# Six raw weight buffers instead of four, and three split tiles instead of four, in a two-block transformer kernel

## The chip, the cores and the metric

One NeuronCore of a Trainium2 chip. The metric is the device time of one execution in microseconds. PE is TensorE (matrix products), DVE is VectorE, ACT is ScalarE, POOL is GpSimd, SP the engine whose queue issues the weight loads.

## What is computed

256 tokens of width 1024, all in float32, pass through two blocks. The first has two layers, each a half-weighted SwiGLU FFN (width 2816), a mixer (attention with convolution in layer 0, a gated recurrence in layer 1) and a second FFN. The second block modulates each part by a condition (shift, scale and gate), and has a mixer and a dense FFN, then a mixer and a mixture of eight experts, of which each token takes two. The parts that fill the time are all of this form:

```python
def _swiglu_2(h, w_gate, w_up, w_down):
    return (jax.nn.silu(h @ w_gate) * (h @ w_up)) @ w_down
```

## The kernel before

**Split products.** PE does not multiply float32 at full precision in one pass, so each weight is split in two: ACT copies it to the reduced format (`wh`, the high part, line 222 as called from `split`), and DVE subtracts that from the original (`wl`, the low part, line 231). The tokens are split in the same way. `mm3` (lines 327 to 336) makes three products of them: high by high (L333), low tokens by high weight (L334), high tokens by low weight (L336).

**Pieces.** Weights come in pieces of 1 MB, 128 partitions by 2048 columns. `load` (L298 to L301) takes a buffer of the pool `raw` and issues the transfer on SP's queue (L300). `split` takes one `wh` and one `wl` tile from their pools and fills them, in parts of 1024 columns in the dense stages and in one of 2048 in the MoE. A raw buffer is free when DVE has read it; a pair of split tiles is free when PE has made the last product of it. Each pool hands out its buffers in turn, so the load of a piece waits for DVE to finish the piece four before it, and the split of a piece waits for PE to finish the piece four before it. In the stages that have spare memory (`ext`), one or two named slots extend the rotation: in `f10`, `f20` and `f11` a fifth pair joins the four, and `self.turn` counts the rotation.

**Stages.** f10, mx0, f20, f11, mx1, f21 (first block), b0, d0, b1, e1 (second). In a dense stage the tokens are two tiles of 128 (tile 0 and tile 1). An FFN runs over six chunks of its width (five of 512, one of 256): up and gate products, the activation, transposes, and the down products of the chunk before. In the first chunk of an FFN and in the first block of a mixer, four pieces are held while PE works tile 0 through all of them, then transposes tile 1's norm (`split_T`, L399), then works tile 1 through the four. An output projection does the same with its four pieces, tile 0 first, whose norm for the next stage then runs on DVE, ACT and POOL while PE works tile 1.

**MoE.** Each expert has 33 pieces. Experts with up to 64 tokens work with "half" blocks: high and low parts of the tokens stand side by side, so that a 1024-by-512 product needs two matmuls per 128 rows (`prod`, L428), 8 for a piece, and `glu` adds the two halves (a copy on ACT, a matmul on PE at L437). One expert of up to 128 tokens works with full blocks, 12 matmuls for a piece. The largest has room for a full block and a half block (12 + 8 = 20 matmuls for a piece); its six chunks are called between those of the others (`big_up`, `big_down`), four or two pieces at a time, so PE passes from 20 matmuls a piece to 8 twelve times. Which expert comes is known at run time alone; the order of work is fixed.

**Order on the engines.** Each engine runs its instructions in one fixed order, which a scheduler writes from the program's order and the buffers' releases. A change of a pool's size can therefore move instructions. There is no table of numbers by hand around the pools, only a few pins.

Of the kernel before, what the change touches and what calls it, by code (L numbers as in the profile page):

```python
# [192 lines left out]
class K:  # L193
    def __init__(self, ctx, tc, A, out, dbg=None):
        self.tc, self.nc, self.A, self.out, self.dbg = tc, tc.nc, A, out, dbg or {}
        e = ctx.enter_context
        self.raw_p = e(tc.tile_pool(name="raw", bufs=4))
        self.h_p = e(tc.tile_pool(name="wh", bufs=4))
        self.l_p = e(tc.tile_pool(name="wl", bufs=4))
        self.slots = e(tc.tile_pool(name="slots", bufs=1))  # L200
        self.cst = e(tc.tile_pool(name="cst", bufs=1))
        self.sm_p = e(tc.tile_pool(name="sm", bufs=1))
        self.ps = e(tc.tile_pool(name="ps", bufs=4, space=bass.MemoryType.PSUM))
        self.dr = e(tc.tile_pool(name="dr", bufs=1, space=bass.MemoryType.DRAM))
        self.n = 0
        self.ext, self.turn, self.in_moe, self.c_row = (), 0, False, None
        self.first, self.behind = True, None
        self.setup()
# [97 lines left out]
    def split(self, raw, nk, n, pin=False):  # L306

        out = []
        if self.turn < 4:
            pair = self.h_p.tile([128, 2048], F32R, tag="wh", name="wh"), self.l_p.tile([128, 2048], F32R, tag="wl", name="wl")  # L310
        else:
            pair = [self.slot(i, [128, 2048], F32R) for i in self.ext]
        self.turn = (self.turn + 1) % (5 if len(self.ext) == 2 else 4)
        hi, lo = pair
        per = nk if self.in_moe else max(1, 1024 // n)
        for k0 in range(0, nk, per):
            m = min(per, nk - k0)
            sl = slice(k0 * n, (k0 + m) * n)
            with self.tc.issue_after(self.behind.ins) if self.behind else ExitStack():
                self.act(hi[:, sl], raw[:, sl], AF.Copy)  # L320
            self.behind = None
            ins = self.tt(lo[:, sl], raw[:, sl], hi[:, sl].bitcast(F32), OP.subtract)
            if pin:
                self.pin(ins)
            out.append([tuple(v[:, k * n:(k + 1) * n] for v in pair) for k in range(k0, k0 + m)])
        return out
# [1554 lines left out]
```

## Time and profile before

| | |
|---|---|
| time of three runs | 2278.87, 2285.14, 2280.76 us; median 2280.76 |
| the profiled execution | 2283.6 us, of which the span from first to last instruction is 2281.8 |
| granted TensorE clock, mean | 0.991 of full speed |
| PE busy | 2174.7 us (95%) |
| DVE, ACT, POOL busy | 1661.9 (73%), 1303.8 (57%), 100.3 us (4%) |
| read from memory | 569.80 MB, 250 GB/s over the span |
| weight loads in the MoE | 264 of 1024 KB, 5.8 us from issue to landing in the median |

In the rows below a line such as `ACT wh L222 <- PE acc L428: 25.3, 12, 5.3` says that ACT sat idle before writing a `wh` tile until a product of line 428 was done, for 25.3 us in all, in 12 cases, at most 5.3 us. A timeline row gives the start, the length, the engine, the line and the operation, how many such instructions were run together (x2), and in brackets the idle time before it with what ended it.

### The profile page before, as it was taken

The numbers are of one execution on the slowest core, as the hardware profiler recorded it, in microseconds if no ns is written. First come the engines' busy times: TensorE is split into PE (matmuls) and PEld (weight loads), VectorE is DVE, ScalarE is ACT, GpSimd is POOL, SyncE is SP. The second block draws the span as 40 slices with busy tenths as digits, with TensorE's granted clock in tenths as the row PEclk, the third lists the DMA queues.
The fourth block names the chain that finished last, engine by engine and source line by source line (L and its number), as shares of the span: only waits on it lengthen the run. The fifth ranks groups of instructions, "written<-read, shape, count | busy, mean of one in ns | idle before, by whom it ended". The sixth has DMA issues, their size and how long they took to land.

```text
span 2281.8 us, 28012 instructions
## 1 busy us (share of the span) xinstructions
PE 2174.7 (95%) x10654; PEld 1752.4 (77%) x10654; DVE 1661.9 (73%) x1900; ACT 1303.8 (57%) x1589; POOL 100.3 (4%) x152
## 2 busy tenths in 40 slices
PE   8999999999999999999999999988999989899997
PEld 6888878888889788877888878756787666676674
DVE  5785967657657876665745666888788788887887
ACT  5455554444437644455544474777666666767675
POOL 0001010000000100120000211000000000000000
PEclk9999999999999999999999999999999999999999
DMA  8684248758755587533655432789898888889886
GB/s 325 251 331 168 104 179 328 265 185 313 274 188 171 200 314 259 207 107 129 231 185 178 165 139 102 286 331 350 295 334 321 324 324 317 328 310 341 317 313 254
DMA packets 82253, 572.82 MB, mean 251 GB/s; under 512 B 9373, under 2 KB 9685, under 8 KB 15424
## 3 DMA queue, kind: packets, MB, share of 16 engines
q1 hardware_dynamic: 77616, 556.73, 65.9%
q0 software_dynamic: 3920, 13.12, 1.8%
q8 instruction: 86, 1.41, 0.2%
q10 hardware_dynamic: 576, 1.11, 0.1%
q14 instruction: 55, 0.45, 0.1%
HBM read 569.80 MB, written 1.12 MB: 250 GB/s over the span
## 4 chain that ended last, share of the span: by engine, by line
PE 39%; DVE 9%; ACT 6%; issue 2%; DMA 1%; POOL 1%; ACTq 0%; DVEq 0%; POOLq 0%
PE mm L428 8%; DVE wl L231 7%; ACT wh L222 5%; PE mm L333 4%; PE mm L334 4%; PE mm L336 4%; PE acc L428 3%; PE acc L334 3%; PE acc L333 3%; PE acc L336 2%; DMA raw<-in_moe 1%; PE mm L1470 1%; ACT s L222 1%; PE mm L596 1%; PE mm L1585 1%
## 5 line engine op out<-in xcount | busy, mean ns | idle before, releaser
L231 DVE TENSOR_TENSOR wl<-raw,wh 128x1024 fp32r<-128x1024 f32 (+3 forms) x658 | 1065.9, 1644 | 356.5 <-ACT wh L222 354.5
L222 ACT ACTIVATE wh<-raw 128x1024 fp32r<-128x1024 f32 (+3 forms) x658 | 897.1, 1393 | 451.5 <-PE mm L334 196.0
L333 PE MATMUL mm<-wh,s 128*128 128x512 f32 (+2 forms) x1144 | 428.5, 380 | 1.6 <-ACT s L222 1.3
L334 PE MATMUL mm<-wh,s 128*128 128x512 f32 (+2 forms) x1144 | 425.3, 376 | 1.5 <-DVE s L231 1.5
L222 ACT ACTIVATE s<-mm 128x512 fp32r<-128x512 f32 (+10 forms) x445 | 225.5, 523 | 346.3 <-PE mm L428 117.0
L336 PE MATMUL mm<-wl,s 128*128 128x512 f32 (+2 forms) x1144 | 322.2, 376 | 1.9 <-DVE wl L231 1.9
L428 PE MATMUL mm<-wl,s 128*128 128x512 f32 (+1 forms) x656 | 248.6, 386 | 32.6 <-DVE wl L231 32.2
L333 PE MATMUL acc<-wh,s 128*128 128x512 f32 x680 | 270.1, 398 | 4.7 <-DVE s L231 2.8
L334 PE MATMUL acc<-wh,s 128*128 128x512 f32 x680 | 268.4, 395 | 0.8 <-DVE s L231 0.8
L333 PEld LDWEIGHTS mm<-wh,s 128*128 128x128 f32 x1144 | 216.8, 190 | 42.4 <-ACT s L222 3.1
L334 PEld LDWEIGHTS mm<-wh,s 128*128 128x128 f32 x1144 | 217.2, 190 | 40.6 <-DVE s L231 3.8
L428 PE MATMUL mm<-wh,s 128*128 128x512 f32 (+1 forms) x656 | 244.1, 380 | 0.0
L336 PEld LDWEIGHTS mm<-wl,s 128*128 128x128 f32 x1144 | 208.1, 190 | 40.6 <-DVE wl L231 2.3
L336 PE MATMUL acc<-wl,s 128*128 128x512 f32 x680 | 213.8, 393 | 0.0
L428 PEld LDWEIGHTS mm<-wl,s 128*128 128x128 f32 x656 | 124.0, 189 | 73.4 <-DVE wl L231 51.0
L333 PEld LDWEIGHTS acc<-wh,s 128*128 128x128 f32 x680 | 128.6, 190 | 32.9 <-ACT s L222 4.2
L334 PEld LDWEIGHTS acc<-wh,s 128*128 128x128 f32 x680 | 129.2, 190 | 27.1 <-DVE s L231 1.7
L336 PEld LDWEIGHTS acc<-wl,s 128*128 128x128 f32 x680 | 128.5, 190 | 26.5
L428 PEld LDWEIGHTS mm<-wh,s 128*128 128x128 f32 x656 | 124.3, 189 | 24.2 <-issue 3.8
L428 PE MATMUL acc<-wl,s 128*128 128x512 f32 x308 | 125.4, 411 | 16.6 <-DVE wl L231 16.6
L231 DVE TENSOR_TENSOR s<-mm,s 128x512 fp32r<-128x512 f32 (+5 forms) x209 | 119.7, 597 | 25.2 <-PE mm L437 12.5
L428 PE MATMUL acc<-wh,s 128*128 128x512 f32 x308 | 125.8, 411 | 2.1 <-ACT wh L222 2.1
(313 smaller groups left out, 2128.0 us busy)
## 6 DMA issues: line engine op xcount, KB each, us to landing
raw<-in_moe SPq DMA_DIRECT2D x264, 1024.0 KB, 5.8
raw<-in_f SPq DMA_DIRECT2D x132, 1024.0 KB, 6.0
raw<-in_ada_w SPq DMA_DIRECT2D x48, 1024.0 KB, 4.9
raw<-in_dense SPq DMA_DIRECT2D x33, 1024.0 KB, 4.8
raw<-in_w_in SPq DMA_DIRECT2D x12, 1024.0 KB, 4.9
raw<-in_ow_in SPq DMA_DIRECT2D x8, 1024.0 KB, 5.0
raw<-in_w_out SPq DMA_DIRECT2D x8, 1024.0 KB, 4.8
raw<-in_ew_in SPq DMA_DIRECT2D x7, 1024.0 KB, 5.0
```

Of the source, the lines that this page charges most:

```text
L222: return self.nc.scalar.activation(out=out, in_=in_, func=func, **kw)
L231: return self.nc.vector.tensor_tensor(out=out, in0=in0, in1=in1, op=op)
L333: mm(out=out, lhsT=xs[i][0], rhs=ws[i][0], start=first and i == 0, stop=False)
L334: mm(out=out, lhsT=xs[i][1], rhs=ws[i][0], start=False, stop=False)
L336: mm(out=out, lhsT=xs[i][0], rhs=ws[i][1], start=False, stop=last and i == n - 1)
L428: self.nc.tensor.matmul(out=out, lhsT=x[0], rhs=w[j][:, c0:c0 + n], start=first and k == 0 and j == 0, stop=last and k == len(ws) - 1 and ...
L596: mm(out=out, lhsT=a, rhs=b, start=j == 0, stop=j == len(todo) - 1)
L1470: mm(out=p[:, k * w:(k + 1) * w], lhsT=h[t][:, a, kk * 128:(kk + 1) * 128], rhs=one[:, o:o + w], start=t == 0, stop=t == 1)
L1585: mm(out=p, lhsT=o[:, t * 128:(t + 1) * 128], rhs=v[:, sl], start=b == 0, stop=b == len(parts) - 1)
```

## The change

The pool `raw` has six buffers instead of four, and the pools `wh` and `wl` have three tiles instead of four. All tiles are 128 by 2048 of 4 bytes, 8 KB of each partition, so the memory is the same: 4 + 4 + 4 and 6 + 3 + 3. The rotation in `split` is shortened by one to match: a split waits for PE to finish the piece three before it (four in f10, f20 and f11, five before), a load waits for DVE to finish the piece six before it.

```diff
-        self.raw_p = e(tc.tile_pool(name="raw", bufs=4))
-        self.h_p = e(tc.tile_pool(name="wh", bufs=4))
-        self.l_p = e(tc.tile_pool(name="wl", bufs=4))
+        self.raw_p = e(tc.tile_pool(name="raw", bufs=6))
+        self.h_p = e(tc.tile_pool(name="wh", bufs=3))
+        self.l_p = e(tc.tile_pool(name="wl", bufs=3))
...
-        if self.turn < 4:
+        if self.turn < 3:
...
-        self.turn = (self.turn + 1) % (5 if len(self.ext) == 2 else 4)
+        self.turn = (self.turn + 1) % (4 if len(self.ext) == 2 else 3)
```

The scheduler writes another order with it. The first place is PE at the start of e1, where the four pieces are `wh_10959`, `wh_10965`, `wh_10971` and `wh_10977` (each with the `wl` of the next number), `mm_10982` and `mm_11007` are tile 0's sums, `mm_11077` is one of tile 1's, and `mm_11039` and `mm_11048` are the transposes of tile 1's norm. Before:

```order
L334 MATMUL mm_11007<-wh_10977,s1_205_10843 128x512
L336 MATMUL mm_11007<-wl_10978,s0_204_10842 128x512 x4
L399 MATMUL mm_11039<-ident_81,s11_206_10844 128x128 x4
L399 MATMUL mm_11048<-ident_81,s11_206_10844 128x128 x4
L1391 MATMUL mm_11058<-rtr_7051,s0_204_10842 128x16 x4
L333 MATMUL mm_11077<-wh_10959,s0_204_10842 128x512
```

With the change, PE around the same transposes:

```order
L336 MATMUL mm_11007<-wl_10972,s0_216_10842 128x512 x4
L399 MATMUL mm_11039<-ident_81,s11_218_10844 128x128 x4
L399 MATMUL mm_11048<-ident_81,s11_218_10844 128x128 x4
L1391 MATMUL mm_11058<-rtr_7051,s0_216_10842 128x16 x8
L1391 MATMUL mm_11058<-rtr_7051,s1_217_10843 128x16 x4
L333 MATMUL mm_11077<-wh_10959,s0_216_10842 128x512
```

The transposes follow the third piece now, without the fourth. Where the fourth comes in on PE, some 15 rows on:

```order
L336 MATMUL mm_11077<-wl_10960,s0_216_10842 128x512 x4
L333 MATMUL mm_11077<-wh_10965,s0_216_10842 128x512
L334 MATMUL mm_11077<-wh_10965,s1_217_10843 128x512
L333 MATMUL mm_11077<-wh_10965,s0_216_10842 128x512
L334 MATMUL mm_11077<-wh_10965,s1_217_10843 128x512
L333 MATMUL mm_11077<-wh_10965,s0_216_10842 128x512
L333 MATMUL mm_11007<-wh_10977,s0_216_10842 128x512
L334 MATMUL mm_11007<-wh_10977,s1_217_10843 128x512
```

Tile 0's products of the fourth piece (`wh_10977`) stood ahead of the transposes; they stand behind tile 1's twelve products of the first piece (`wl_10960` ends them) and five of the second. The starts of f21, b0, d0 and b1 change in the same way.

The second place is PE in the output projection of b1, ahead of e1, where the four pieces are `wh_10756`, `wh_10764`, `wh_10772` and `wh_10780`, `acc_10750` and `acc_10751` are tile 0's sums, and `acc_10752` and `acc_10753` tile 1's. Before, on PE, the end of the fourth piece for tile 0 and the beginning of tile 1:

```order
L333 MATMUL acc_10751<-wh_10780,s3_195_10448 128x512
L334 MATMUL acc_10751<-wh_10780,s10_196_10449 128x512
L336 MATMUL acc_10751<-wl_10781,s3_195_10448 128x512 x2
L333 MATMUL acc_10752<-wh_10756,s3_195_10448 128x512
L334 MATMUL acc_10752<-wh_10756,s10_196_10449 128x512
```

Tile 1 began when tile 0 had used all four. With the change, on PE, the fourth piece's beginning for tile 0:

```order
L333 MATMUL acc_10753<-wh_10764,s3_207_10448 128x512
L334 MATMUL acc_10753<-wh_10764,s10_208_10449 128x512
L333 MATMUL acc_10753<-wh_10764,s3_207_10448 128x512
L334 MATMUL acc_10753<-wh_10764,s10_208_10449 128x512
L336 MATMUL acc_10753<-wl_10765,s3_207_10448 128x512
L333 MATMUL acc_10751<-wh_10780,s3_207_10448 128x512
L334 MATMUL acc_10751<-wh_10780,s10_208_10449 128x512
L333 MATMUL acc_10751<-wh_10780,s3_207_10448 128x512
```

The fourth piece of tile 0 moved behind tile 1's work on the first piece and five products of the second. The transposes of tile 0's norm for e1 follow later (`mm_10858`, `mm_10867`). Before, on PE, near the projection's end:

```order
L333 MATMUL acc_10753<-wh_10764,s3_195_10448 128x512
L334 MATMUL acc_10753<-wh_10764,s10_196_10449 128x512
L399 MATMUL mm_10858<-ident_81,s11_206_10844 128x128 x4
L333 MATMUL acc_10753<-wh_10764,s3_195_10448 128x512
L399 MATMUL mm_10867<-ident_81,s11_206_10844 128x128 x4
L1391 MATMUL mm_10877<-rtr_7051,s0_204_10842 128x16 x4
```

One product of tile 1 stood between the two, and more behind. With the change, on PE:

```order
L333 MATMUL acc_10753<-wh_10780,s3_207_10448 128x512
L334 MATMUL acc_10753<-wh_10780,s10_208_10449 128x512
L336 MATMUL acc_10753<-wl_10781,s3_207_10448 128x512 x2
L399 MATMUL mm_10858<-ident_81,s11_218_10844 128x128 x4
L399 MATMUL mm_10867<-ident_81,s11_218_10844 128x128 x4
L1391 MATMUL mm_10877<-rtr_7051,s0_216_10842 128x16 x4
```

They stood among tile 1's products of the projection, and now stand behind its last one. The output projection of b0 changes alike. In the steady chunks of an FFN and in the half blocks of the MoE PE's order is nearly the same as before, and the weight loads stand in the same order among themselves.

## Rows read from the trace of the kernel before

**Rows 1.** busy time by stage (us from:to, its length, then by engine, clock, DMA share, GB/s)

```profile
100.00:1350.00 1250.00, 1230.93 (x6339) 1036.05 (x6337) 853.24 (x1199) 627.86 (x954) 87.79 (x125) 1.00 0.58 211
...
1490.00:2282.00 792.00, 720.03 (x3225) 535.82 (x3223) 645.44 (x448) 537.59 (x441) 0.00 (x0) 0.99 0.85 319
```

**Rows 2.** waits of ACT, 1490 to 2282 us (us in total, times, longest us)

```profile
ACT s L222 <- PE mm L428: 112.2, 62, 4.8
ACT wh L222 <- PE acc L428: 25.3, 12, 5.3
ACT wh L222 <- DMA raw<-in_moe: 22.6, 27, 2.2
```

**Rows 3.** waits of the load queue, 1490 to 2282 us

```profile
SPq L300 <- DVE wl L231: 530.8, 205, 7.6
```

**Rows 4.** waits of DVE and of PE, 1490 to 2282 us

```profile
DVE wl L231 <- ACT wh L222: 98.6, 87, 5.9
...
PE mm L428 <- DVE wl L231: 30.2, 32, 1.8
```

**Rows 5.** chain of waits, 1490 to 2282 us, by engine and line

```profile
by line: PE mm L428 20.6%; DVE wl L231 17.9%; ACT wh L222 10.4%; PE acc L428 8.1%; PE mm L333 5.3%; PE mm L336 5.1%; PE mm L334 5.1%; issue 4.5%; DMA raw<-in_moe 3.6%; PE acc L334 2.5%; PE acc L333 2.4%; PE acc L336 2.3%; PE mm L1470 2.3%; 
```

**Rows 6.** PE, timeline at five stage starts (start us, us, work, [idle before])

```profile
782.26 1.04 PE L399 MATMUL mm<-ident,s 128*128 128x128 f32 x8
...
973.43 1.23 PE L399 MATMUL mm<-ident,s 128*128 128x128 f32 x8 [1.65 <-DVE s L231]
...
1103.63 1.03 PE L399 MATMUL mm<-ident,s 128*128 128x128 f32 x8
...
1291.64 1.03 PE L399 MATMUL mm<-ident,s 128*128 128x128 f32 x8
...
1416.53 0.39 PE L333 MATMUL mm<-wh,s 128*128 128x512 f32 x1
...
1419.25 1.03 PE L399 MATMUL mm<-ident,s 128*128 128x128 f32 x8
```

**Rows 7.** splits by shape, 100 to 900 us: DVE, ACT (busy us, mean ns | idle before)

```profile
L231 DVE TENSOR_TENSOR wl<-raw,wh 128x1024 fp32r<-128x1024 f32 x228 | 271.7, 1220 | 128.9 <-ACT wh L222 128.7
...
L222 ACT ACTIVATE wh<-raw 128x1024 fp32r<-128x1024 f32 x228 | 231.8, 1053 | 219.4 <-PE mm L334 99.9 <-PE acc L334 77.5 <-DMA raw<-in_f 29.2
```

**Rows 8.** DVE, timeline: last step of the norms ahead of those transposes

```profile
777.79 1.42 DVE L239 SCALAR_TENSOR_TENSOR s<-x,sy,s 128x512 f32<-128x512 f32 x2 [0.73 <-POOL sy L381]
...
972.60 1.29 DVE L231 TENSOR_TENSOR s<-s,s 128x512 f32<-128x512 f32 x2
...
1100.65 1.28 DVE L231 TENSOR_TENSOR s<-s,s 128x512 f32<-128x512 f32 x2
...
1289.48 1.28 DVE L231 TENSOR_TENSOR s<-s,s 128x512 f32<-128x512 f32 x2
...
1398.12 1.28 DVE L231 TENSOR_TENSOR s<-s,s 128x512 f32<-128x512 f32 x2
...
1417.28 1.29 DVE L231 TENSOR_TENSOR s<-s,s 128x512 f32<-128x512 f32 x2
```

**Rows 9.** PE, timeline: token tile 0's transposes ahead of e1

```profile
1398.95 0.63 PE L399 MATMUL mm<-ident,s 128*128 128x128 f32 x4 [0.87 <-DVE s L231]
```

**Rows 10.** ACT, timeline of the turns at 1800 and at 2026 us

```profile
1791.64 5.73 ACT L222 ACTIVATE wh<-raw 128x2048 fp32r<-128x2048 f32 x3
...
2025.95 1.92 ACT L222 ACTIVATE wh<-raw 128x2048 fp32r<-128x2048 f32 x1 [4.34 <-PE acc L428]
2030.48 3.73 ACT L222 ACTIVATE wh<-raw 128x2048 fp32r<-128x2048 f32 x2 [2.61 <-PE acc L428]
```

**Rows 11.** DVE, timeline of the turn at 2026 us

```profile
2042.76 9.02 DVE L231 TENSOR_TENSOR wl<-raw,wh 128x2048 fp32r<-128x2048 f32 x4
```

**Rows 12.** PE, timeline of the turn at 1800 us

```profile
1799.79 0.39 PE L428 MATMUL mm<-wl,s 128*128 128x512 f32 x1
...
1805.08 0.39 PE L428 MATMUL mm<-wh,s 128*128 128x512 f32 x1
```

## The prediction

> **What bounds the kernel now.** I read four views in this order: busy time by stage, the waits of the MoE stage, its chain of waits, and the timelines of the places where the number of split tiles decides.
>
> Busy time by stage [rows 1] shows two regimes. From 100 to 1350 us PE is busy 1230.93 of 1250 us: what delays a weight there is hidden while PE has a split tile in hand, and only a gap in PE costs. In the MoE, 1490 to 2282 us, PE is busy 720.03 of 792, DVE 645.44, ACT 537.59, and the DMA share is 0.85: four resources, none full all the time.
>
> The MoE's waits tell which one is short when. ACT waits 22.6 us for weights to land and 25.3 us for a split tile that PE still reads in its accumulating half products, but 112.2 us for half-block sums to copy [rows 2]. The load queue waits 530.8 us, 205 times, until DVE has read a raw buffer [rows 3]: the loads run against their four buffers nearly always. DVE waits 98.6 us for ACT, and PE only 30.2 us for DVE's low parts in the half blocks' up products [rows 4]. In the chain of waits of the same stretch, landing weights hold 3.6% (28.5 us of 792), DVE's low parts 17.9%, ACT's high parts 10.4%, and products most of the rest [rows 5].
>
> **The change, part by part.** It adds and removes no operation; it changes when a load may start (six pieces unread by DVE instead of four) and when a split may start (after PE has released piece k-3, not k-4). Total buffered pieces rise from 8 to 9. No term for busy time.
>
> **Steady dense FFN: nothing.** There a piece serves both token tiles, 24 matmuls of 0.227 us (12 take from 1416.53 to 1419.25 [rows 6]), so 5.4 us. Splitting one takes ACT two times 1.05 us and DVE two times 1.22 us [rows 7]. With three tiles PE has two pieces, 10.8 us, in hand while the third is refilled. If that cover went, each piece would show a gap in PE; I find no place for it.
>
> **Five stage starts: +9 us.** The stages f21, b0, d0, b1 and e1 begin with four pieces held at once: PE works token tile 0 through all four, then transposes tile 1's norm (L399), then works tile 1. With three tiles the fourth piece can only be split after tile 1 has used the first, so the transposes come one product earlier, which is 12 matmuls or 2.72 us [rows 6]. The norm must be there that much earlier, or PE waits. PE can transpose about 0.83 us after DVE begins the last step of the norm: 1398.12 [rows 8] to 1398.95 [rows 9]. From the five transposes [rows 6] and the five norm steps [rows 8]:
> f21: wanted at 782.26 - 2.72 = 779.54, the norm there at 777.79 + 0.8 = 778.6: 0.
> b0: it waited 1.65 already, so all 2.72 is lost: 2.7.
> d0: 1100.65 + 0.83 = 1101.48 against 1100.91: 0.6.
> b1: 1290.31 against 1288.92: 1.4.
> e1: 1418.11 against 1416.53: 1.6.
> Together 6.3. Then PE has only four or five matmuls of the second piece (about 1 us) while the fourth is split: with 1.05 us for ACT's first half and 1.22 for DVE's [rows 7] I charge 0.5 in four stages, and 0.8 in e1, where ACT splits a whole 2048 columns in 1.92 [rows 10]: 2.8. Sum 9.1. Lower bound 2 (DVE reaches the norm earlier, since the fourth split no longer stands ahead of it); upper bound 5 x (2.72 + 1.0) = 19.
>
> **Two output projections before d0 and e1: +2 us.** Their fourth piece too moves behind tile 1's work on the first. Tile 0's norm then finishes later, and its transposes come behind the last product instead of among them. Today PE waits 0.87 us there [rows 9]; that goes, and a bare chain of transposes, ACT copy and DVE low part comes, of which I charge 1 us each. Bounds 0 and 4.
>
> **Turns in the MoE: +7 us.** Twelve times PE passes from a large expert's blocks, 20 matmuls (4.5 us) a piece, to half blocks, 8 matmuls (1.8 us) a piece, which is less than the 2.26 us that DVE needs for one (four in 9.02 [rows 11]). What has been split ahead is then used up, and one tile less counts. The hardest turn is at 2026 us. ACT starts its splits as PE releases tiles, at 2025.95 and 2030.48, after idle times of 4.34 and 2.61 [rows 10]. With three tiles each of these starts one release later: that of 2025.95 at about 2030.5, that of 2030.48 at about 2032.3, and so on. DVE, which does four splits without a pause from 2042.76 to 2051.78 [rows 11], leaves that run up to 3.7 us late. About 1.7 comes back behind it, where a load waited for its raw buffer. So +2.0 net. The turn at 1800 us shows the easy case. ACT makes three splits from 1791.64 on [rows 10], and with three tiles the third waits until PE leaves the large block, at 1800.1; it is ready 1.92 + 2.26 later, at 1804.4, while PE comes to it at 1805.08 [rows 12]: nothing lost. The other four turns that I followed release by release gave 0.2, 0.2, 0.4 and 0.7. Mean 0.6, times 12: 7. Bounds 0 and 12 x 3.7 = 44.
>
> **Six raw buffers: -11 us.** They can take away ACT's 22.6 us of waiting for weights [rows 2]. In the half-block runs ACT does its work in a written order and then mostly waits for sums (112.2 us), so an earlier landing is often followed by another wait: I take half. Bounds 0 and -28.5, the share of landing in the chain [rows 5]. Before the MoE a later or earlier landing is covered by PE's work.
>
> Sum: 9 + 2 + 7 - 11 = **+7 us** on the profiled execution of 2283.6, 2290.6. The median of the three runs shown is 2280.76, 2.8 lower, and I forecast against it: **2288 us**. A difference under 0.3%, 6.8 us, is about what a measurement of this kernel cannot tell from none, so this lies just at that line.
>
> A rule to weigh against this: the sum takes PE as the engine that decides where it is 91% busy in the MoE [rows 1]. The Trainium skill, page "Perfetto Trace Analysis", section "Identifying the Most-Contended Engine", says that PE's matmul busy share is no good measure of its headroom, and wants the busy share of weight loads. By that rule PE in the MoE is at 535.82 of 792, 68%, below DVE at 81%, and DVE and the loads would be what to look at. The sum by it would be that of the first rival.
>
> **The rivals.**
> 1. Faster: the loads bind the MoE. For: 205 waits for a raw buffer [rows 3], a DMA share of 0.85, and 28.5 us of landing in the chain [rows 5]. Against: ACT found its piece not landed only 27 times, and for 22.6 us in all [rows 2]. Then all 28.5 comes back, the turns cost nothing because the loads run ahead in the large blocks, and the starts cost 9: -20, 2261 us. The same page, section "Optimization Strategy", says that a gap repeating on the engine that should be saturated can mean too few buffers. The load queue's 205 waits agree with that as a pattern; that this queue is the one to saturate is what the 22.6 us speak against.
> 2. Much slower: the split tiles bind at every turn as at 2026 us. It decides as soon as PE, after a turn, has less left in hand than one split takes, 1.92 + 2.26 = 4.2 us. Then 12 x 3.7 = 44 stands for 7: +44, 2325 us; if at half of the turns, +25, 2306. For: 12 waits of ACT for L428's accumulating products, mean 2.1 us, longest 5.3 [rows 2]. Against: in five of the six turns that I followed PE had that much.
> 3. No change: three tiles do all that four did, and the raw buffers fill time that nobody waits for; the 2.7 us steps at the starts are met by norms that finish earlier. 2281 us. For: PE waits for DVE's low parts only 30.2 us there [rows 4]. Against: b0 has no slack at all, its transposes wait already [rows 6].
>
> **How the numbers follow.** Forecast case (-1 to +16 us) 0.41; faster 0.20; much slower 0.20; no change 0.19. The forecast case lies about two fifths within 0.3%, the rest above. So faster by over 0.3%: 0.20; within: 0.19 + 0.16 = 0.35; slower: 0.25 + 0.20 = 0.45. The range reaches to the middle of the first rival, 2261, and a little past the half-way form of the second, 2312, leaving out about one in ten on each side.
>
> **What would show it.** In the changed profile: at the five starts the transposes in L399 stand 2.7 us nearer to the stage's first product, with a wait for DVE of 1 to 4 us ahead of them in b0, b1 and e1. ACT's wait for landing weights in the MoE falls below 8 us, and the load queue's waits for DVE shrink. ACT's waits for L428's accumulating products rise from 25 us. Busy times stay within 1%. I am wrong if the MoE stretch changes by more than 15 us either way, or if the stretch from 750 to 1490 us does not grow by 5 to 15.

## The result and the profile after

The changed kernel takes 2301.41 us in the median of four runs (2295.81 to 2302.76), the kernel before 2281.78 beside it (four runs). The ratio is 1.0081, with an interval of 1.0058 to 1.0103: slower by 0.8%, some 19 us. The same kernel in a second series gave 2300.75 against 2281.39, ratio 1.0081 [1.0055, 1.0106]. The forecast was 2288: the sign and most of the places were right, and more than half of the loss was not in its sum.

The first line to read in the profile after is PE's. PE has as many products as before and is busy 17.9 us longer, while the span grew by 19.2 (2281.8 to 2301.0).

```profile
PE 2192.6 (95%) x10654; PEld 1760.0 (76%) x10654; DVE 1663.1 (72%) x1900; ACT 1305.1 (57%) x1589; POOL 103.9 (5%) x152
```

Where the time came from is seen by cutting both runs at the same pieces of work. This is the busy time by stage of the kernel before, with the columns of [rows 1]:

```profile
100.00:696.00 596.00, 590.99 (x3012) 496.60 (x3011) 424.42 (x616) 277.59 (x412) 20.76 (x34) 1.00 0.64 234
696.00:957.00 261.00, 256.92 (x1344) 219.01 (x1342) 187.52 (x243) 141.85 (x195) 13.75 (x23) 1.00 0.65 236
957.00:1061.00 104.00, 98.38 (x539) 80.99 (x540) 67.28 (x117) 64.03 (x133) 24.41 (x30) 0.97 0.40 141
1061.00:1277.00 216.00, 214.04 (x1047) 178.84 (x1045) 119.16 (x138) 95.92 (x131) 8.34 (x16) 1.00 0.49 176
1277.00:1374.50 97.50, 95.10 (x540) 78.88 (x541) 66.45 (x114) 62.77 (x129) 22.18 (x25) 1.00 0.42 151
1374.50:1411.10 36.60, 35.71 (x200) 29.79 (x199) 24.27 (x37) 18.59 (x32) 3.33 (x7) 1.00 0.23 84
1411.10:1523.60 112.50, 101.40 (x485) 77.33 (x483) 90.83 (x124) 78.23 (x73) 2.79 (x4) 0.97 0.77 287
1523.60:1654.00 130.40, 120.47 (x554) 90.42 (x554) 104.74 (x73) 92.34 (x81) 0.00 (x0) 0.97 0.86 322
1654.00:2281.80 627.80, 572.84 (x2552) 427.34 (x2552) 514.33 (x360) 421.06 (x341) 0.00 (x0) 0.99 0.85 317
```

And this is that of the changed kernel:

```profile
100.00:697.40 597.40, 592.86 (x3015) 496.93 (x3014) 426.22 (x621) 276.56 (x413) 21.85 (x34) 1.00 0.64 235
697.40:961.70 264.30, 258.49 (x1344) 219.96 (x1342) 186.55 (x242) 142.02 (x195) 12.03 (x23) 0.99 0.64 231
961.70:1066.70 105.00, 98.87 (x539) 81.24 (x540) 67.03 (x117) 63.70 (x133) 24.35 (x30) 0.97 0.39 140
1066.70:1285.50 218.80, 215.27 (x1047) 178.51 (x1045) 119.86 (x138) 96.22 (x131) 8.79 (x16) 1.00 0.49 174
1285.50:1386.20 100.70, 96.64 (x540) 80.28 (x541) 65.99 (x114) 62.59 (x129) 23.74 (x25) 0.98 0.42 146
1386.20:1427.60 41.40, 38.65 (x200) 31.89 (x199) 26.14 (x39) 18.87 (x34) 6.01 (x8) 0.92 0.29 102
1427.60:1540.10 112.50, 103.19 (x485) 78.42 (x483) 91.65 (x124) 80.54 (x73) 2.25 (x4) 0.95 0.75 286
1540.10:1673.60 133.50, 124.48 (x554) 93.83 (x554) 104.89 (x74) 92.77 (x81) 0.00 (x0) 0.95 0.82 310
1673.60:2301.00 627.40, 576.04 (x2552) 426.35 (x2552) 514.60 (x360) 422.59 (x341) 0.00 (x0) 0.99 0.83 314
```

PE's counts agree row by row within 3, so each pair is the same work. Up to 1411 us (1427.6 in the changed kernel) lie the dense stages with the stage starts and output projections. These six rows grew by 1.4, 3.3, 1.0, 2.8, 3.2 and 4.8: 16.5 us. The three rows of the MoE grew by 0, 3.1 and -0.4: 2.7. PE's idle time, a row's length less its busy time, grew by 6.9 in the six rows and fell by 6.3 in the three. The granted clock is lower in five of the nine rows, most in the sixth, 0.92 against 1.00, and in the seventh and eighth.

To price the clock I cut each profiled run into windows of 4 us and added PE's busy time times (1 - granted clock): 17.3 us before, 28.2 after (with windows of 8 us 16.4 and 27.0). That is 10.9 of the 19.2 us, 5.7 ahead of the MoE's second piece and 5.2 behind it. It is a bound from above where PE was not the engine waited for. By this estimate the starts and projections cost 16.5 - 5.7 = 10.8 without the clock, and the MoE gave 2.7 - 5.2 = -2.5. PE's busy time grew by 7.0 more than the clock explains. A product is recorded with 0.39 us and the next can follow after 0.227 [rows 6], so a wait of up to 0.16 us between two products shows as busy time. That the 7.0 are such waits is likely, and not shown here.

The starts themselves, in PE's timeline (beside [rows 6] and [rows 9]), with the projection of mx1 in the first row:

```profile
760.86 1.74 PE L333 MATMUL acc<-wh,s 128*128 128x512 f32 x4 [2.59 <-ACT s L222]
...
783.48 1.03 PE L399 MATMUL mm<-ident,s 128*128 128x128 f32 x8
...
977.80 1.23 PE L399 MATMUL mm<-ident,s 128*128 128x128 f32 x8 [2.42 <-DVE s L231]
...
1108.88 1.23 PE L399 MATMUL mm<-ident,s 128*128 128x128 f32 x8 [1.57 <-DVE s L231]
...
1298.40 1.23 PE L399 MATMUL mm<-ident,s 128*128 128x128 f32 x8 [0.83 <-DVE s L231]
...
1417.56 1.17 PE L399 MATMUL mm<-ident,s 128*128 128x128 f32 x8 [1.29 <-DVE s L231]
...
1421.47 1.02 PE L1391 MATMUL mm<-rtr,s 128*128 128x16 f32 x4 [1.31 <-DVE s L231]
1422.35 0.77 PE L334 MATMUL mm<-wh,s 128*128 128x512 f32 x1
1422.92 0.63 PE L333 MATMUL mm<-wh,s 128*128 128x512 f32 x1
1423.35 0.63 PE L334 MATMUL mm<-wh,s 128*128 128x512 f32 x1
```

The transposes of f21 do not wait, those of b0, d0 and b1 do, and ahead of e1 there are now two pauses, one for tile 0's transposes (1417.56) and one for its router products (1421.47). Behind the second the products last 0.63 us and follow each other after 0.43 (1422.92 to 1423.35). At full clock they last 0.39 and follow after 0.227 [rows 6]: PE is at the lower of its two levels, 1.2 GHz instead of 2.4. In windows of 4 us the same place reads:

```profile
1416.00:1420.00 4.00, 2.56 (x19) 1.92 (x17) 4.00 (x6) 3.59 (x4) 0.00 (x0) 1.00 0.60 246
1420.00:1424.00 4.00, 2.69 (x11) 2.31 (x11) 3.15 (x4) 0.31 (x1) 0.00 (x0) 0.52 0.57 172
1424.00:1428.00 4.00, 4.00 (x13) 3.33 (x14) 3.33 (x5) 0.72 (x2) 1.67 (x1) 0.62 0.21 90
```

PE was busy 2.56 of 4 us while DVE was busy all of them, and 2.69 of the next 4; there and in the third window, where PE is busy throughout, the clock is 0.52 and 0.62.

In the MoE the waits of ACT, of the load queue and of PE, and the chain of waits, are to be held against [rows 2] to [rows 5]:

```profile
ACT s L222 <- PE mm L428: 81.5, 51, 3.6
ACT wh L222 <- PE mm L428: 56.5, 28, 4.5
ACT wh L222 <- PE acc L428: 30.3, 17, 7.1
...
SPq L300 <- DVE wl L231: 552.1, 211, 8.0
...
PE mm L428 <- DVE wl L231: 31.3, 32, 1.8
...
by line: PE mm L428 23.2%; DVE wl L231 14.8%; ACT wh L222 11.6%; PE acc L428 9.5%; PE mm L333 5.2%; PE mm L336 5.1%; PE mm L334 5.0%; issue 4.3%; PE mm L1585 4.1%; PE acc L334 2.6%; PE acc L333 2.6%; PE acc L336 2.6%; PE mm L1470 2.4%; PE m
```

ACT's wait for landing weights, 22.6 us before [rows 2], is out of the list, and landing is out of the chain, where it held 3.6% [rows 5]. ACT waits in its stead for a split tile that PE still reads: 56.5 us for L428's half products into `mm`, a wait that had 10.4 us before:

```profile
ACT wh L222 <- PE mm L428: 10.4, 5, 4.3
```

The load queue waits as much as before, 552.1 us against 530.8 [rows 3].

### The profile page after: what moved, and what is told of

The parts are those of the page before. It is cut to its first block, busy times and chain, and to the rows that moved or that the text cites. A ratio compares the mean times of both kernels' runs of the same rounds, so it can differ in the third digit from the quotient of the medians.

```text
span 2301.0 us, 27931 instructions
## 1 busy us (share of the span) xinstructions
PE 2192.6 (95%) x10654; PEld 1760.0 (76%) x10654; DVE 1663.1 (72%) x1900; ACT 1305.1 (57%) x1589; POOL 103.9 (5%) x152
## 4 chain that ended last, share of the span: by engine, by line
PE 41%; DVE 8%; ACT 6%; issue 2%; POOL 1%; ACTq 0%; DVEq 0%; POOLq 0%
PE mm L428 9%; DVE wl L231 6%; ACT wh L222 5%; PE mm L333 4%; PE mm L334 4%; PE mm L336 4%; PE acc L428 4%; PE acc L333 2%; PE acc L334 2%; PE acc L336 2%; PE mm L1585 1%; PE mm L1470 1%; ACT s L222 1%; DVE s L231 1%; PE mm L596 1%
## 5 line engine op out<-in xcount | busy, mean ns | idle before, releaser
L231 DVE TENSOR_TENSOR wl<-raw,wh 128x1024 fp32r<-128x1024 f32 (+3 forms) x646 | 1051.6, 1652 | 336.0 <-ACT wh L222 333.5
L222 ACT ACTIVATE wh<-raw 128x1024 fp32r<-128x1024 f32 (+3 forms) x646 | 887.8, 1400 | 539.8 <-PE mm L334 257.1
L333 PE MATMUL mm<-wh,s 128*128 128x512 f32 (+2 forms) x1144 | 422.5, 376 | 1.7 <-ACT s L222 1.3
L334 PE MATMUL mm<-wh,s 128*128 128x512 f32 (+2 forms) x1144 | 419.3, 373 | 0.7 <-DVE s L231 0.6
L222 ACT ACTIVATE s<-mm 128x512 fp32r<-128x512 f32 (+9 forms) x445 | 225.4, 523 | 259.1 <-PE mm L428 81.8
L336 PE MATMUL mm<-wl,s 128*128 128x512 f32 (+2 forms) x1144 | 315.1, 372 | 2.1 <-DVE wl L231 2.1
L428 PE MATMUL mm<-wl,s 128*128 128x512 f32 (+1 forms) x656 | 252.6, 392 | 32.0 <-DVE wl L231 31.3
L333 PE MATMUL acc<-wh,s 128*128 128x512 f32 (+1 forms) x656 | 259.6, 398 | 5.5 <-ACT s L222 3.3
L334 PE MATMUL acc<-wh,s 128*128 128x512 f32 (+1 forms) x656 | 259.0, 395 | 0.6 <-DVE s L231 0.5
L428 PE MATMUL mm<-wh,s 128*128 128x512 f32 (+1 forms) x656 | 247.4, 385 | 0.5 <-ACT s L222 0.5
L336 PE MATMUL acc<-wl,s 128*128 128x512 f32 (+1 forms) x656 | 208.4, 394 | 0.0
L428 PEld LDWEIGHTS mm<-wl,s 128*128 128x128 f32 x656 | 125.8, 192 | 72.9 <-DVE wl L231 50.6
L333 PEld LDWEIGHTS acc<-wh,s 128*128 128x128 f32 x656 | 124.1, 190 | 32.5 <-ACT s L222 5.3
L428 PEld LDWEIGHTS mm<-wh,s 128*128 128x128 f32 x656 | 126.1, 192 | 27.4 <-issue 4.7
L334 PEld LDWEIGHTS acc<-wh,s 128*128 128x128 f32 x656 | 124.5, 190 | 27.0 <-DVE s L231 2.3
L428 PE MATMUL acc<-wl,s 128*128 128x512 f32 x308 | 125.4, 412 | 13.9 <-DVE wl L231 13.7
L231 DVE TENSOR_TENSOR s<-mm,s 128x512 fp32r<-128x512 f32 (+5 forms) x209 | 119.8, 597 | 25.2 <-PE mm L437 12.5
L428 PE MATMUL acc<-wh,s 128*128 128x512 f32 x308 | 127.5, 416 | 0.8 <-DVE s L231 0.5
```

Source lines behind the costliest of these rows:

```text
L222: return self.nc.scalar.activation(out=out, in_=in_, func=func, **kw)
L231: return self.nc.vector.tensor_tensor(out=out, in0=in0, in1=in1, op=op)
L333: mm(out=out, lhsT=xs[i][0], rhs=ws[i][0], start=first and i == 0, stop=False)
L334: mm(out=out, lhsT=xs[i][1], rhs=ws[i][0], start=False, stop=False)
L336: mm(out=out, lhsT=xs[i][0], rhs=ws[i][1], start=False, stop=last and i == n - 1)
L428: self.nc.tensor.matmul(out=out, lhsT=x[0], rhs=w[j][:, c0:c0 + n], start=first and k == 0 and j == 0, stop=last and k == len(ws) - 1 and ...
```

## The experiments

The theory after the result (A in the texts on record) was that the loss lies at the stage starts and the projections, where the fourth split now stands behind tile 1's work. Its rivals were that the three tiles bind at the MoE's turns (B), and that two more loads in flight disturb other work (C). A later rival, D, shared the place with A, but held that the MoE gains nothing when e1's start alone is repaired.

To change one stage alone, the pools were made 4 raw, 3 `wh` and 3 `wl`, and two named slots of the same size serve either as a fourth pair of split tiles or as fifth and sixth raw buffers. A function says which sizes hold (digits: raw, `wh`, `wl`), and `mp` counts the pieces that the MoE has split. Where "444" holds, the order on the engines is that of before: in the first run below PE's first 7154 products, up to 1430 us, are the same, line by line. The kernel's lines lie somewhat further down (L222 is L223, L428 is L442).

```diff
+    def sizes(self):
+        return "633" if self.mp >= 4 else "444"
...
-        raw = self.raw_p.tile([128, 2048], F32, tag="raw", name="raw")
+        raw = self.rot(self.raw_p, self.nr, int(k[0]), 4, {"433": [], "444": [], "633": [20, 21], "543": [21], "534": [20]}[k], F32, "raw")
```

The table gives all runs, each with the kernel before beside it. "Profiled" is the span of the profiled run less the 2281.8 of before; "clock" is how far the sum of busy time times (1 - granted clock) differs from before's 17.3; "rest" is the one less the other. The profiled run need not be a middle one: for the change in the dense stages it took 2303.14 us, the least of four, and for three split tiles with four raws 2308.51, the most of five.

| kernel | median us (runs) | before | ratio [95%] | profiled | clock | rest |
|---|---|---|---|---|---|---|
| the change | 2301.41 (4) | 2281.78 | 1.0081 [1.0058, 1.0103] | +19.2 | +10.9 | +8.3 |
| the change again | 2300.75 (6) | 2281.39 | 1.0081 [1.0055, 1.0106] | +16.6 | +10.2 | +6.4 |
| change in the MoE alone | 2277.5 (12) | 2282.2 | 0.9969 [0.9957, 0.9982] | -8.7 | -7.8 | -0.9 |
| change in dense stages alone | 2309.11 (4) | 2282.2 | 1.0121 [1.0102, 1.014] | +19.5 | +7.4 | +12.1 |
| three split tiles, four raws | 2304.33 (5) | 2282.2 | 1.009 [1.0074, 1.0107] | +24.9 | +8.9 | +16.0 |
| the same in the MoE alone | 2287.32 (12) | 2282.2 | 1.0024 [1.0014, 1.0034] | +3.8 | -1.5 | +5.3 |
| four tiles at b1's and e1's start | 2300.2 (6) | 2282.66 | 1.0074 [1.0052, 1.0096] | +18.1 | +4.9 | +13.2 |
| one pause filled | 2293.94 (8) | 2282.66 | 1.005 [1.0033, 1.0067] | +12.5 | +5.0 | +7.5 |
| MoE with 5, 4 and 3 | 2284.04 (12) | 2282.66 | 1.0006 [0.9993, 1.0019] | -0.9 | +1.4 | -2.3 |
| MoE with 5, 3 and 4 | 2278.94 (12) | 2282.66 | 0.9989 [0.9972, 1.0005] | -7.3 | -7.8 | +0.5 |
| both of e1's pauses filled | 2297.77 (6) | 2281.39 | 1.0071 [1.0043, 1.01] | +9.5 | -1.4 | +10.9 |

**Which stage: the change in the MoE alone.** The edit is the function above: "633" from the MoE's fifth piece on, "444" ahead of it.

> Six raw buffers and three split tiles only in the MoE, after its first four pieces; four and four before that (two of the tiles serve as the fourth split pair first and as two raw buffers later). Theory A, the loss lies where four pieces are held at once (five stage starts and two output projections), because the fourth split waits: 1 to 5 us over the kernel before, about 2284. Rival B, the loss lies in the MoE's turns: 12 to 20 us over, about 2298.

Measured: 0.9969 [0.9957, 0.9982], so faster than before, by 4.7 us between the medians (7.1 by the ratio). B falls; A's 1 to 5 us over the kernel before is missed too, on the other side. ACT's waits, 1487 to 2273 us:

```profile
ACT s L223 <- PE mm L442: 77.7, 51, 3.1
ACT wh L223 <- PE mm L442: 56.5, 27, 4.5
ACT wh L223 <- PE acc L442: 29.2, 17, 5.9
```

They are close to those of the changed kernel (81.5, 56.5, 30.3). The MoE with six raws and three tiles does the same here, and the whole is faster than before: what the change loses, it loses ahead of this stage or because of what happened there. Most of the gain of the profiled run is a higher clock, -7.8 of -8.7. Of the 8.7 us, 2.5 stand ahead of 1411 us, where both kernels run the same order; the verdict rests on the twelve runs, all but one at a clock of 0.993 to 0.995, and not on that profile.

**The converse: the change in the dense stages alone.**

```diff
+        return "444" if self.mp >= 4 else "633"
```

> The reverse: six raw buffers and three split tiles up to the MoE's first four pieces, four and four after them. Theory A: about 16 us over the kernel before, about 2298, with the same steps at f21, b0, d0, b1 and e1 in the trace as the change shows. Rival B: 0 to 6 us over.

Measured: 1.0121 [1.0102, 1.014], 26.9 us between the medians where A expected 16. All of the loss is here, and more. Part of the excess is this kernel's own: in mx1 PE waits 5.16 us for a high part, which it does neither before nor in the change. That the shared slots cause it is likely and not shown. The wait is this one:

```profile
743.05 1.65 PE L610 MATMUL acc<-s,wh 128*128 128x256 f32 x6 [5.16 <-ACT wh L223]
```

**The raw buffers: three split tiles with four raws, throughout and in the MoE alone.**

```diff
+        return "433"
```

> Three split tiles with the four raw buffers of before, everywhere. Theory A: the same 16 us up to the MoE's start, since raw buffers play no part there, and in the MoE the cost of the turns without what the loads give back: 10 to 25 us, in all 26 to 42 over the kernel before, about 2308 to 2324. Rival C, the loss at the starts comes from six loads in flight, which delay the row transfers that the norms wait for: no loss up to the MoE's start, in all 10 to 25 over.

```diff
+        return "433" if self.mp >= 4 else "444"
```

> As the first, but with four raw buffers and three split tiles in the MoE. It prices the two halves of the change in the MoE: the difference to the first run is what two more raw buffers give back. My working of before has 7 for the turns and 11 for the loads: then this is 7 us over the kernel before, about 2289, and the first 4 under it. If the loads give back all of ACT's waits for landing weights, 22 us more than the first run.

Measured: 1.009 [1.0074, 1.0107] throughout, with the starts as late as in the change: 4.7 us late at 957 and at 1061 us (the change 4.7 and 5.7), 8.9 at 1277 (8.5), 12.1 at 1374 (11.7). With no load more in flight than before the loss is the same, so C falls. A's 26 to 42 us in all was too much; it came to 22.1. In the MoE alone three tiles with four raws cost 1.0024 [1.0014, 1.0034], 5.5 us (5.1 between the medians); this is what the turns cost, where 7 was expected. The two further raws are the difference between this kernel and the first: 9.8 us between the medians, 12.5 between the profiled spans, of which 6.3 is clock. ACT's wait for landing weights is down to 8.5 us already with four raws:

```profile
ACT wh L223 <- DMA raw<-in_moe: 8.5, 14, 1.0
```

**One start repaired: four tiles in b1 and at e1's start.**

```diff
+        if self.stage in ("b1", "e1") and self.mp < 4:
+            return "444"
+        return "633"
```

> The change, but with four raw buffers and four split tiles in b1 and for the MoE's first four pieces. Theory A (pauses of PE where four pieces are held, and a lower granted clock behind each): of the change's loss, the 7 us at b1's output projection and e1's start go, and the MoE, entered with PE at full speed, gains as in the first run: 2282 + 9 at f21, b0 and d0 - 7 in the MoE = 2282 to 2288. Rival D, the MoE's gain in the first run comes from the dense stages being left as they were (clock or order): the MoE gains nothing, 2290 to 2296.

Measured: 1.0074 [1.0052, 1.0096], 2300.2 us, which is neither's. From 1277 to 1411 us the lateness goes from 12.6 to 12.8, where the change loses 8.0 more (8.5 to 16.5): the repair works at its place. But the kernel has two waits of its own, in mx1 and where it goes back to "633":

```profile
743.41 1.65 PE L612 MATMUL acc<-s,wh 128*128 128x256 f32 x6 [5.13 <-ACT wh L223]
...
1459.36 0.79 PE L444 MATMUL mm<-wh,s 128*128 128x512 f32 x1 [4.70 <-ACT wh L223]
```

They take the gain away, so the total decides nothing.

**The clock: e1's pause filled.** The change unaltered, but ahead of tile 0's first up products PE makes eight products whose result the first real one overwrites. DVE's work, which PE waits for there, is the same.

```diff
                 banks[j] = self.mm()
+                for d in range(8 if j == t == 0 else 0):
+                    mm(out=banks[j], lhsT=xT[0][:, t, d % 4], rhs=up0[0][0][d % 4][0], start=True, stop=True)
```

> The change, with eight matmuls more that compute nothing (0.23 us each) in the pause of PE at e1's start, behind the transposes of tile 0. If the pause itself makes the clock fall, the granted clock of 0.52 and 0.62 from 1420 to 1428 us rises to near 1, and the stretch from the transposes to the end of the first piece's products is 2 to 3.5 us shorter though it has more work. If the clock falls for another reason, that stretch stays or grows by up to 1.8 us. In the whole: -3 to +2 us.

Measured: 2293.94 us, 7.5 less than the change, with more work, where 3 less was the most expected. In windows of 4 us and in PE's timeline:

```profile
1416.00:1420.00 4.00, 2.56 (x17) 1.73 (x15) 3.86 (x6) 2.94 (x3) 0.10 (x1) 1.00 0.73 262
1420.00:1424.00 4.00, 4.00 (x26) 3.50 (x25) 3.89 (x4) 1.06 (x2) 0.00 (x0) 1.00 0.31 86
1424.00:1428.00 4.00, 4.00 (x20) 3.33 (x21) 3.64 (x6) 0.72 (x2) 1.97 (x1) 1.00 0.42 176
...
1421.00 1.61 PE L1412 MATMUL mm<-wh,s 128*128 128x512 f32 x6
...
1426.11 0.40 PE L333 MATMUL mm<-wh,s 128*128 128x512 f32 x1
...
1432.60 1.23 PE L399 MATMUL mm<-ident,s 128*128 128x128 f32 x8 [0.87 <-DVE s L231]
```

PE pauses as long between 1416 and 1420, but not after, and the clock stays at 1.00. From the transposes (1418.31 here, 1417.56 in the change) to the last product of the first piece (1426.11; 1427.59) it takes 7.8 us instead of 10.0, though eight products of 0.23 us, 1.8 us, have come in. At this place the low clock came with the pause: with the pause filled it is gone. The second profile of the change has the low clock there too (0.65 and 0.50 from 1416 to 1424 us), and that of the next experiment, with the pause filled, has none.

Yet the 2.2 us did not last. PE, sooner at tile 1's transposes, now waits 0.87 us for DVE ahead of them (1432.60), where the change has no wait, and at 1523 us of the kernel before, by equal products, this run is 16.4 us late and the change 16.5. So the clock's price at e1's start went into other waits, and the gain of the profiled run (12.5 late at the end, where the change has 19.2) came after it: by 1654 us the two are 14.3 and 19.6 late. Between the two places the clock fell for a shorter time than in the change; nothing was edited there, and why it did is not shown.

**Both pauses of e1 filled** (`8 if j == 0`, so tile 1 has its eight products too).

> The change with eight idle matmuls behind the transposes of tile 0 and eight behind those of tile 1 at e1's start (the sixth run had the first eight alone). If PE's pauses bring the lower clock, the slow stretch behind tile 1's transposes (0.67 from 1438 to 1442 us in the change) goes too: 1 to 3 us under the sixth run, 2290 to 2293, at a mean clock of 0.990 or more. If the sixth run's gain came from something else: as the sixth or up to 2 us slower.

Measured: six runs in two groups, 2293.03 to 2294.1 at a mean clock of 0.991 or 0.992, and 2301.43 to 2303.65 at 0.987 or 0.988. The better half is where the runs with one filled pause were; the other is as slow as the change. The 2290 to 2293 expected was just missed by the better half and by far by the other, and the second filling gives nothing that can be seen. Nor does a filled pause make the gain sure, since three of these six runs do not have it. The time follows the clock from run to run of the same program, and it does so in the kernel before: over 59 runs of it, the 17 at 0.993 and 0.994 took 2275.8 to 2281.6 us, the 6 at 0.987 and 0.988 took 2286.5 to 2292.2. Yet with 2298.19 at the lowest of six runs and clocks of 0.985 to 0.988, the change repeated never had one of the better half's:

> The change unaltered, as the base for the next run on the same chip: 17 to 22 us over the kernel before, at a mean granted clock of 0.985 to 0.988.

Measured: 1.0081 again. The lateness at 1061, 1277 and 1374 us is 2.8, 5.5 and 8.7, which is 2.9 or 3.0 less than in the first profiled run at each; what it lacks was lost before 957 us. By 1411 us it is 13.5 late, where the first had 16.5.

**Other divisions in the MoE.** Three tiles for the low parts alone, or for the high parts alone:

```diff
+        return "543" if self.mp >= 4 else "444"
```

> As the first run, but five raw buffers, four high tiles and three low tiles in the MoE. If the loads' gain comes with the fifth buffer and ACT may run ahead with four high tiles: 2272 to 2278, below the first run. If the low tiles decide alone: the same turn cost as with three, and half of the loads' gain, 2280 to 2284.

```diff
+        return "534" if self.mp >= 4 else "444"
```

> The mirror of the seventh: five raw buffers, three high tiles, four low tiles in the MoE. ACT's split waits for PE as with three of both, so it should be no better than five raw buffers with three and three: 2280 to 2285.

Measured: 1.0006 [0.9993, 1.0019] and 0.9989 [0.9972, 1.0005], both the same as before within their intervals. The first, 2284.04, is at the upper edge of what was expected if the low tiles decide; the second, 2278.94, is 1 us under its 2280 to 2285, so its reason, that ACT's split waits as with three of both, is not borne out. Six, three and three in the MoE alone is the only version that is clearly faster than the kernel before; its interval overlaps that of five, three and four.

## Why the prediction was right or wrong

**The step that failed** is the sentence "No term for busy time", and the whole sum's pricing of a pause as the time for which PE stands still. The sum was +7. By the estimate without the clock the two profiled runs of the change measured +8.3 and +6.4. The term that was missing is the lower granted clock, at most +10.9 and +10.2, which the change brought along: all ten runs of it have a mean clock of 0.985 to 0.988, while the kernel before has 0.987 to 0.994 in 59. The prediction had the row for it: [rows 1] give 0.99 for the MoE, with products at 1.00 elsewhere, and it asked neither where the missing hundredth was nor what PE had done ahead of it.

**Stage starts and projections, forecast 9 + 2 = 11.** Measured 16.5, of which 5.7 is clock: 10.8 for the waits, of which 6.9 shows as idle time of PE. In the first row, 100 to 697 us, stand 1.4 of it, where the forecast has no place; the second profile of the change has nothing there. By their parts the terms are less exact. f21 was costed at nothing for its transposes and has no wait. b0 was to lose all of 2.72 and waits 2.42 where it waited 1.65. d0 and b1, forecast 0.6 and 1.4, wait 1.57 and 0.83. In e1 the forecast was a wait of 1.6 ahead of tile 1's transposes; there is none there, and the two pauses stand a tile earlier, 1.29 for the norm and 1.31 for the router products, for which it had 1 us. Ahead of the router products' low part DVE made the split of a MoE piece (128x2048, 2.28 us from 1418.54), which the text did not have. Nor did it have the pause of 2.59 in mx1's projection, against 0.69 before. That the sum agrees is partly luck.

**Turns, forecast 7 (0 to 44).** Measured by themselves, 5.5, and 5.3 without the clock. The small mean of the turns that were followed release by release held; 3.7 us at every turn, the upper bound, did not come.

**Six raws, forecast -11 (0 to -28.5).** Measured -9.8 between the medians and -12.5 between the profiled spans, half of the latter clock. The reason given, half of ACT's wait for landing, is only partly right: that wait went altogether, and ACT's time went into waiting for split tiles instead, while its wait for half-block sums fell from 112.2 to 81.5. Three tiles alone cut it from 22.6 to 8.5, presumably because splits start later then.

**The MoE as a whole, forecast -4.** 2.7 in the change, -2.5 without the clock; alone it is faster by 4.7 (medians). Why the same stage has a higher clock when the starts ahead of it are those of before is not shown. That the stage is entered with other waits and so pauses elsewhere is a guess.

**The signs to look for.** Right: transposes one product nearer; ACT's landing wait below 8 us; its waits for L428's accumulating products up, 30.3 from 25.3; busy times of PE, DVE and ACT within 1%, though PE's 0.8% was the matter (POOL's grew by 3.6%, 100.3 to 103.9); the MoE within 15 us. From 696 to 1411 us the growth was 15.1, at the upper end of the 5 to 15 given for much the same stretch. Wrong: of the waits of 1 to 4 us in b0, b1 and e1 only b0's came, and the load queue's waits did not shrink. It runs against its buffers with six as with four, so the length of that queue's waits says nothing of what its buffers are worth.

**The rivals.** The first, the loads bind the MoE, falls as a whole, but its mechanism is what the MoE-alone kernel gains by. The Trainium skill, "Perfetto Trace Analysis", section "Optimization Strategy", says that a gap repeating on the engine that should be saturated can mean too few buffers. Here 205 such gaps of the load queue, 530.8 us of them, were worth about 10 us to two more buffers. The same page of the Trainium skill, section "Identifying the Most-Contended Engine", would have looked past PE in the MoE. The runs do not bear that out there, for with landing out of the chain PE's L428 has 23.2% of it, where it had 20.6. The second rival, every turn like the worst, falls by the 5.5 us. Its half-way form, 2306, landed nearer in total than the forecast, for another reason; its full form, 2325, did not. The first rival's own sum leaves out the projections' 2: by the prediction's terms it gives -17.5 and not -20. The third, no change, falls by the waits at the starts.

## What to carry to other kernels

A pause of PE can have two prices, its length and the clock behind it; where PE is the bound, look at the granted clock just behind each pause that a change makes or moves, and compare PE's busy time at equal counts, which holds short waits too (17.9 us here, of which the clock is 10.9). What is saved at one pause has to be followed to the next common place, since a later wait can take it back, as it did at e1's start. A depth of buffers is best chosen by stage: as many processed tiles as pieces held at once where PE holds four of them, more raw buffers where loads are short. And a wait that fills a queue is worth what the next wait behind it leaves over, which is read from the consumer's waits (22.6 us), not from the queue's (530.8).

## What the runs showed of the hardware

Behind a pause of one to three microseconds the clock can be lower, and need not be. Windows of 4 us of the changed kernel, at mx1's projection (a pause of 2.59 us), at d0's transposes (1.57) and at the pause of 1.43 us in an expert of the MoE:

```profile
760.00:764.00 4.00, 3.14 (x8) 2.43 (x9) 4.00 (x6) 3.82 (x5) 0.00 (x0) 0.68 0.45 111
...
1108.00:1112.00 4.00, 2.81 (x14) 1.93 (x15) 2.62 (x5) 1.20 (x2) 0.60 (x1) 1.00 1.01 405
1112.00:1116.00 4.00, 4.00 (x18) 2.98 (x17) 1.57 (x2) 2.01 (x2) 0.00 (x0) 1.00 0.21 87
...
1592.00:1596.00 4.00, 4.00 (x15) 3.52 (x15) 3.18 (x4) 1.24 (x3) 0.00 (x0) 0.50 0.99 373
1596.00:1600.00 4.00, 4.00 (x15) 3.32 (x13) 2.26 (x1) 3.04 (x2) 0.00 (x0) 0.50 0.84 291
1600.00:1604.00 4.00, 4.00 (x12) 3.23 (x13) 2.65 (x3) 0.58 (x1) 0.00 (x0) 0.50 0.77 246
```

In the window of the first the clock is 0.68, at the second it is 1.00, and behind the third PE is busy for all of 12 us at 0.50. The kernel before does the same work of that expert at full clock, behind a pause of 1.42 us:

```profile
1576.00:1580.00 4.00, 4.00 (x28) 3.57 (x27) 3.52 (x3) 3.37 (x4) 0.00 (x0) 1.00 0.89 342
```

28 products in 4 us there, 12 to 15 here. Which pause costs the clock, and for how long, stays open; that the low clock goes when a pause is filled is shown at e1's start alone.
